# A fixed order for the head of a hybrid encoder layer: one root, rescaling by quarters, idle transposes

## The chip, the cores and the metric

The kernel runs on one core of a Trainium2 chip. The metric is device time in microseconds: 1707.37 before, the median of 3 runs (1707.24 to 1707.54).

## The reference

One layer of a bidirectional encoder, in float32, for one sequence of 256 tokens of width 2048. Cut to what matters:

```python
h = concatenate([meta, x])                  # 16 meta tokens ahead of 256 tokens
n = rms_norm(h, norm_mix)                   # n = h * rsqrt(mean(h*h) + eps) * gain
p = n @ w_in                                # 2048 x 15360: inputs of four mixers, and 4 x 2048 gates
z = [rglru(p_a), hyena(p_b), retention(p_c), hgrn2(p_d)]      # 512 wide each
h = h + sum_b(sigmoid(gate_b) * (z_b @ w_branch_out[b])) @ w_out
h = h + (silu(n2 @ w_gate) * (n2 @ w_up)) @ w_down            # n2 = rms_norm(h, norm_ffn)
return rms_norm(h, norm_final)[16:]
```

The change concerns the first `rms_norm` and its transposition, up to the first projections. Each `rms_norm` needs, for each token, the sum of squares over its 2048 columns, a root and a reciprocal before any column can be scaled.

## The kernel before, in words

All matmuls with weights are done in three passes in a reduced float32 format: weight and activation are each split into a rounded part (`hi`, `nh`) and the rest (`lo`, `nl`), and hi x nh, hi x nl and lo x nh are summed. The weights come from memory in pieces of 128 x 1024 (512 KB), four buffers deep, all on SP's DMA queue, in the order in which `piece` (L95) is called. Of each piece ScalarE (ACT) makes `hi` by a copy (L112) and VectorE (DVE) `lo` by a subtraction (L113); for the first two pieces (`NPOOL`) GpSimd (POOL) does both, 1024 columns at once (L110, L113).

The head works like this. `par` holds all small parameters in one tile of 321 columns and is loaded first (L86); then come the meta tokens `xm`, as 128 rows of 256, and x in two row tiles of 128 tokens, each in two halves of 1024 columns (L226, L231). For the meta tile ACT takes the squares (L260), TensorE (PE) sums them over groups of partitions with the matrix `ind` from `par` (L262), `rsqrt` (L159 to L163) makes the factor in three steps on DVE, ACT and DVE, DVE scales `xm` (L266), PE transposes it (L271), and DVE and ACT write it into `nh` and `nl` (L274, L156, L157). For each row tile `squares` takes the four quarters of 512 columns in turn on ACT and DVE, sums them and takes a root for this tile alone; `rescale` multiplies the quarters in place. Then for each of the 16 column blocks k PE transposes the block of both row tiles into one bank of PSUM (L280), ACT writes `nh[k]` with the gain (L281) and DVE `nl[k]` (L282). The first chunk of the projection (`mix_chunk`) takes pieces 0 to 3, with four blocks k each: 6 matmuls for a block, of 272 columns (L312 to L314).

The order on each engine is not the program's. A planner with its own costs places all instructions: at each moment an engine gets the ready instruction that stands first in the program; the pieces from the seventh on are advanced by 250 places. On the chip each engine then works in this order. Explicit edges without a semaphore (`tc.add_manual_dep`, `tc.issue_after`) put one instruction behind another on the same engine. POOL also issues the DMAs of `mlp` (the inputs of the Hyena filter network, read by `sines` within `filters`, L196) and `rope` (read by `rotate` in mixer C, L688).

Of the kernel before, what the change touches and what calls it, by code (L numbers as in the profile page):

```python
# [10 lines left out]
F32 = mybir.dt.float32  # L11
# [6 lines left out]
P = 128  # L18
D = 2048
# [11 lines left out]
GU_HALF = (6, 5)  # L31
NS, NH, NT = 7, 6, 8
NPOOL = 2
WPAD = 64
WAHEAD = 250
MAGIC = 12582912.0
# [20 lines left out]

PCOL = {}
_n = 0
for _name, _w in (("norm_mix", 16), ("norm_ffn", 16), ("lcw", 16), ("lcb", 4), ("lba", 8), ("lbx", 8), ("lam", 8),  # L60
                  ("hcw", 36), ("hcb", 12), ("hbias", 4), ("lb", 4), ("b1", 1), ("b2", 1), ("dec", 8),
                  ("negt", 2), ("nyq", 1), ("ind", P), ("fill", 48)):
    PCOL[_name] = _n
    _n += _w
NPAR = _n
# [2 lines left out]
def body(tc, a, out):  # L68
# [14 lines left out]
        return psp.tile(list(shape), F32, tag="ps", name=name)  # L83

    par = const.tile([P, NPAR], F32, name="par")
    nc.sync.dma_start(par, a["par"])  # L86

    def pc(name, i=0, rows=P):
        return par[:rows, PCOL[name] + i:PCOL[name] + i + 1]

    ident = const.tile([P, P], F32, name="ident")
    make_identity(nc, ident)

    wpos = [0]
    first = []  # L95

    def piece(kt, cols, dst=None, skip=0):

        i = wpos[0]
        wpos[0] += 1  # L100
        with tc.high_priority(offset=WAHEAD if i >= 6 else 0):
            raw = rawp.tile([P, kt, cols], F32, tag="raw", name="raw")
            nc.sync.dma_start(raw, a["w"][i].rearrange("p (k n) -> p k n", k=kt))
            if dst:
                hi, lo = dst
            else:
                hi, lo = [p.tile([P, 1024 + WPAD], F32R, tag=x, name=x)[:, skip:skip + 1024]
                          .rearrange("p (k n) -> p k n", k=kt) for p, x in ((hip, "hi"), (lop, "lo"))]
            if i < NPOOL:
                G.tensor_scalar(hi, raw, 1.0, 0.0, op0=MUL, op1=ADD)  # L110
            else:
                A.copy(hi, raw)  # L112
            ins = (G if i < NPOOL else V).tensor_tensor(lo, raw, hi.bitcast(F32), op=SUB)  # L113
            if i == 1:
                first.append(ins.ins)
        return hi, lo
# [76 lines left out]


    mlp = H("mlp", 128 + T, rows=64)
    G.dma_start(mlp, a["mlp"])  # L196
    f2 = mc.tile([P, T], F32, name="f2")

    def sine(dst, src, bias):
# [8 lines left out]
        A.activation(dst, x, AF.Sin)  # L208

    def sines():  # L210
        p1 = ps("pf1")
        PE.matmul(p1[:64, :T], mlp[:33, 0:64], mlp[:33, 128:], start=True, stop=True)
        f1 = TT("f1", T, rows=64)
        sine(f1, p1[:64, :T], pc("b1", rows=64))
        p2 = ps("pf2")
        PE.matmul(p2[:64, :T], mlp[:, 64:128], f1, start=True, stop=True)
        sine(f2[:64], p2[:64, :T], pc("b2", rows=64))
        G.memset(f2[64:], 0.0)
# [9 lines left out]
    for t in range(2):  # L228
        halves = [zp.tile([P, 1024], F32, tag=f"z{2 * t + i}", name=f"x{t}_{i}") for i in range(2)]
        for i in range(2):  # L230
            nc.sync.dma_start(halves[i], a["x"][t * P:t * P + P, i * 1024:i * 1024 + 1024])  # L231
        xts.append(halves)
    ss = tiny("ss", 3, 4)
    rs = tiny("rs", 3)

    def quarter(g, q):
        return xts[g][q // 2][:, q % 2 * 512:q % 2 * 512 + 512]

    def squares(g, engs):
        for q, e in enumerate(engs):  # L240
            dump = H("dump", 512)
            x, acc = quarter(g, q), ss[:, g, q:q + 1]
            if e == "A":
                A.activation(dump, x, AF.Square, accum_out=acc)
            else:
                V.scalar_tensor_tensor(dump, x, 1.0, x, op0=MUL, op1=MUL, accum_out=acc)
        r = rs[:, g:g + 1]
        V.tensor_reduce(r, ss[:, g], op=ADD, axis=mybir.AxisListType.X)
        rsqrt(r, r, 1.0 / D)

    def rescale(g, engs):
        for q, e in enumerate(engs):
            x, r = quarter(g, q), rs[:, g:g + 1]
            if e == "A":
                A.activation(x, x, AF.Copy, scale=r)
            else:
                V.tensor_scalar(x, x, r, None, op0=MUL)

    dump = H("dump", 256)
    A.activation(dump, xm, AF.Square, accum_out=ss[:, 2, 0:1])  # L260
    pm = ps("pmeta")
    PE.matmul(pm[:, 0:1], par[:, PCOL["ind"]:PCOL["ind"] + P], ss[:, 2, 0:1], start=True, stop=True)  # L262
    rsqrt(rs[:, 2:3], pm[:, 0:1], 1.0 / D)
    squares(0, "AVAV")
    squares(1, "AVAV")
    V.tensor_scalar(xm, xm, rs[:, 2:3], None, op0=MUL)  # L266
    rescale(0, "AVAV")
    rescale(1, "VAVA")
    pm = ps("pmeta")
    for b in range(2):  # L270
        PE.transpose(pm[:, b * P:b * P + P], xm[:, b * P:b * P + P], ident)  # L271
# [1 line left out]
    gain = par[:, PCOL["norm_mix"]:PCOL["norm_mix"] + KT].rearrange("p (k b) -> p k b", b=2)  # L273
    V.tensor_tensor(nm, pm[:, 0:256].rearrange("p (b t k) -> p k b t", b=2, k=8),  # L274
                    gain[:, :, :, None].to_broadcast([P, 8, 2, META]), op=MUL)
    split(nh[:, :, 0:META], nl[:, :, 0:META], nm.rearrange("p k b t -> p (k b) t"))
    for k in range(KT):
        pt = ps("ptn")
        for t in range(2):
            PE.transpose(pt[:, t * P:t * P + P], xts[t][k // 8][:, (k % 8) * P:(k % 8) * P + P], ident)  # L280
        anchor = [A.activation(nh[:, k, META:], pt[:, :SEQ], AF.Copy, scale=pc("norm_mix", k)),  # L281
                  V.scalar_tensor_tensor(nl[:, k, META:], pt[:, :SEQ], pc("norm_mix", k), nh[:, k, META:].bitcast(F32),  # L282
                                         op0=MUL, op1=SUB)]

    def late(eng, ins):
        tc.add_manual_dep(ins.ins, anchor[eng].ins.name, mybir.DependencyInfo(
# [398 lines left out]

    def mixer_c():
        rope = H("rope", 2, T)
        G.dma_start(rope, a["rope"])  # L688
        def rotate(x, n):

            y = S("rot", NW, n)
# [485 lines left out]
```

## Time and profile before

| | |
|---|---|
| time, median of 3 runs | 1707.37 us |
| the profiled execution | 1708.65 us, span 1706.9 us |
| chain that ended last, by engine | PE 93%, DVE 4%, ACT 2%, issue 1% |
| mean length of a row tile's `nh` (L281) and `nl` (L282) in the first 36 us | 0.475 us each |
| mean length of a piece's `hi` on ACT and `lo` on DVE | 1.05 and 1.24 us |
| first use of `mlp` by PE, of `rope` by DVE | 57.0 and 173.1 us |
| `mlp`, `rope`: from issue to landing | 5.6 and 7.7 us |

The span runs from the first to the last instruction of the profiled execution; what its own time has beyond the span lies ahead of and behind it. A matmul on PE is pipelined, so that the length shown for one is longer than its distance to the next; the chain of waits shows the distances. The granted clock of PE is given as a share of 2.4 GHz.

### The profile page before, as it was taken

The numbers are of one execution on the slowest core, as the hardware profiler recorded it, in microseconds if no ns is written. First come the engines' busy times: TensorE is split into PE (matmuls) and PEld (weight loads), VectorE is DVE, ScalarE is ACT, GpSimd is POOL, SyncE is SP. The second block draws the span as 40 slices with busy tenths as digits, with TensorE's granted clock in tenths as the row PEclk, the third lists the DMA queues.
The fourth block names the chain that finished last, engine by engine and source line by source line (L and its number), as shares of the span: only waits on it lengthen the run. The fifth ranks groups of instructions, "written<-read, shape, count | busy, mean of one in ns | idle before, by whom it ended". The sixth has DMA issues, their size and how long they took to land.

```text
span 1706.9 us, 22379 instructions
## 1 busy us (share of the span) xinstructions
PE 1667.4 (98%) x8844; PEld 1437.0 (84%) x8844; DVE 954.6 (56%) x1140; ACT 803.8 (47%) x969; POOL 80.6 (5%) x74
## 2 busy tenths in 40 slices
PE   6999999999999999999999999999999999999997
PEld 5999999989978888888888888888888888888886
DVE  6755895486675445454455545454545444544554
ACT  5544465474574444444445544444444334444443
POOL 2000000001002002010020000000000000000001
PEclk9999999999999999999999999999999999999999
DMA  6546444546356555555666555555555555555554
GB/s 238 184 140 193 144 140 145 181 139 212 111 172 211 188 194 186 196 194 188 197 198 210 197 197 186 192 190 187 191 190 188 194 196 190 194 185 190 193 191 142
DMA packets 87225, 313.81 MB, mean 184 GB/s; under 512 B 9824, under 2 KB 10112, under 8 KB 86992
## 3 DMA queue, kind: packets, MB, share of 16 engines
q1 hardware_dynamic: 84960, 304.42, 54.0%
q0 software_dynamic: 2160, 7.97, 1.5%
q8 instruction: 69, 1.13, 0.3%
q14 instruction: 36, 0.29, 0.1%
HBM read 309.17 MB, written 2.10 MB: 182 GB/s over the span
## 4 chain that ended last, share of the span: by engine, by line
PE 93%; DVE 4%; ACT 2%; issue 1%; DMA 0%; SPq 0%; ACTq 0%
PE acc L135 23%; PE acc L136 23%; PE acc L134 23%; PE mix L312 5%; PE mix L314 5%; PE mix L313 5%; DVE lo L113 1%; PE pth L948 1%; PE last L1006 1%; PE last L1005 1%; PE last L1007 1%; DMA x<-in_x_dram 0%; ACT hi L112 0%; PE pl L635 0%; PE pg L801 0%
## 5 line engine op out<-in xcount | busy, mean ns | idle before, releaser
L113 DVE TENSOR_TENSOR lo<-raw,hi 128x1024 fp32r<-128x1024 f32 x556 | 686.5, 1235 | 668.9 <-ACT hi L112 668.6
L112 ACT CAST hi<-raw 128x1024 fp32r<-128x1024 f32 x556 | 585.0, 1053 | 759.9 <-PE acc L136 620.1
L136 PE MATMUL acc<-hi,n2l 128*128 128x512 f32 x704 | 274.0, 389 | 0.0
L135 PE MATMUL acc<-lo,n2h 128*128 128x512 f32 x704 | 273.9, 389 | 0.0
L312 PE MATMUL mix<-nh,hi 128*128 128x272 f32 (+2 forms) x896 | 255.0, 287 | 3.4 <-DVE cg L521 1.8
L314 PE MATMUL mix<-nh,lo 128*128 128x272 f32 (+2 forms) x896 | 252.8, 287 | 4.3 <-DVE lo L113 4.3
L313 PE MATMUL mix<-nl,hi 128*128 128x272 f32 (+2 forms) x896 | 255.9, 287 | 0.0
L134 PE MATMUL acc<-hi,n2h 128*128 128x512 f32 x704 | 249.4, 390 | 0.0
L135 PE MATMUL acc<-lo,nh 128*128 128x512 f32 x512 | 200.1, 391 | 2.8 <-DVE lo L113 2.8
L136 PE MATMUL acc<-hi,nl 128*128 128x512 f32 x512 | 199.8, 390 | 0.0
L134 PE MATMUL acc<-hi,nh 128*128 128x512 f32 x512 | 181.7, 391 | 0.6 <-ACT hi L112 0.6
L312 PEld LDWEIGHTS mix<-nh,hi 128*128 128x128 f32 x896 | 169.9, 190 | 5.9 <-issue 2.8
L314 PEld LDWEIGHTS mix<-nh,lo 128*128 128x128 f32 x896 | 168.6, 190 | 6.1 <-DVE lo L113 5.2
L313 PEld LDWEIGHTS mix<-nl,hi 128*128 128x128 f32 x896 | 170.2, 190 | 0.7 <-issue 0.2
L136 PEld LDWEIGHTS acc<-hi,n2l 128*128 128x128 f32 x704 | 132.1, 188 | 27.5
L134 PEld LDWEIGHTS acc<-hi,n2h 128*128 128x128 f32 x704 | 132.2, 188 | 27.1
L135 PEld LDWEIGHTS acc<-lo,n2h 128*128 128x128 f32 x704 | 132.2, 188 | 27.1
L136 PE MATMUL acc<-hi,hidl 128*128 128x512 f32 x312 | 121.4, 389 | 0.0
L135 PE MATMUL acc<-lo,hidh 128*128 128x512 f32 x312 | 121.4, 389 | 0.0
L135 PEld LDWEIGHTS acc<-lo,nh 128*128 128x128 f32 x512 | 96.1, 188 | 24.0 <-DVE lo L113 4.5
L134 PEld LDWEIGHTS acc<-hi,nh 128*128 128x128 f32 x512 | 96.0, 188 | 20.9 <-ACT hi L112 1.3
L136 PEld LDWEIGHTS acc<-hi,nl 128*128 128x128 f32 x512 | 96.2, 188 | 19.6
(388 smaller groups left out, 1644.7 us busy)
## 6 DMA issues: line engine op xcount, KB each, us to landing
raw<-in_w_dram SPq DMA_DIRECT2D x568, 512.0 KB, 3.3
x<-in_x_dram SPq DMA_DIRECT2D x4, 512.0 KB, 8.7
h<-in_x_dram SPq DMA_DIRECT2D x8, 256.0 KB, 4.2
out_dram<-h SPq DMA_DIRECT2D x8, 256.0 KB, 3.1
lruw<-in_lruw_dram POOLq DMA_DIRECT2D x2, 512.0 KB, 6.3
dm<-in_decay_dram POOLq DMA_DIRECT2D x4, 256.0 KB, 4.3
nf<-in_norm_final_dram POOLq DMA_DIRECT2D x1, 1024.0 KB, 6.6
rot<-ck POOLq DMA_DIRECT2D x2, 272.0 KB, 6.0
```

The lines of the kernel that those rows point to most:

```text
L112: A.copy(hi, raw)
L113: ins = (G if i < NPOOL else V).tensor_tensor(lo, raw, hi.bitcast(F32), op=SUB)
L134: PE.matmul(acc[t], xh[:, k, s], wh[:, j], start=(i + j == 0), stop=False)
L135: PE.matmul(acc[t], xh[:, k, s], wl[:, j], start=False, stop=False)
L136: PE.matmul(acc[t], xl[:, k, s], wh[:, j], start=False, stop=(i + j == n - 1))
L312: PE.matmul(o, wh[:, j, s], nh[:, k, t0:T], start=(k == 0), stop=False)
L313: PE.matmul(o, wh[:, j, s], nl[:, k, t0:T], start=False, stop=False)
L314: PE.matmul(o, wl[:, j, s], nh[:, k, t0:T], start=False, stop=(k == KT - 1))
L948: PE.transpose(pt[:, j * P:j * P + P], s[:, j * P:j * P + P], ident)
L1005: PE.matmul(acc, xh, wh, start=(k == 0), stop=False)
L1006: PE.matmul(acc, xh, wl, start=False, stop=False)
L1007: PE.matmul(acc, xl, wh, start=False, stop=(k == 2 * n - 1))
```

## The change

- `par` is loaded in two parts: `norm_mix`, `ind` first (144 columns), the other 177 columns behind x.
- The squares of both row tiles stand ahead of the sum; one reduction and one `rsqrt` serve both. Edges put these steps, on ACT and on DVE, behind the meta tile's split and in program order.
- Row tile 0 is rescaled on ACT, row tile 1 on DVE, by quarters: quarter 0 ahead of the transposes, quarters 1, 2, 3 behind the blocks k = 1, 5, 9. The `nh` and `nl` of all k are held in order with them.
- 40 transposes of the identity into a bank of PSUM that nobody reads stand behind the meta tile's split in the program.
- POOL converts pieces 0 and 1 in four slices of 256 columns each, `hi` and `lo` in turn.
- The conversions of pieces 2, 3, 4 on ACT and DVE are put behind `nh` and `nl` of k = 5, 9, 13.
- The DMA of `mlp` is issued within `filters`, and that of `rope` too behind POOL's last step of piece 1.

```diff
--- before.py
+++ after.py
@@ -31,6 +31,7 @@
 GU_HALF = (6, 5)
 NS, NH, NT = 7, 6, 8
 NPOOL = 2
+NWARM = 40
 WPAD = 64
 WAHEAD = 250
 MAGIC = 12582912.0
@@ -57,9 +58,9 @@
 
 PCOL = {}
 _n = 0
-for _name, _w in (("norm_mix", 16), ("norm_ffn", 16), ("lcw", 16), ("lcb", 4), ("lba", 8), ("lbx", 8), ("lam", 8),
+for _name, _w in (("norm_mix", 16), ("ind", P), ("norm_ffn", 16), ("lcw", 16), ("lcb", 4), ("lba", 8), ("lbx", 8), ("lam", 8),
                   ("hcw", 36), ("hcb", 12), ("hbias", 4), ("lb", 4), ("b1", 1), ("b2", 1), ("dec", 8),
-                  ("negt", 2), ("nyq", 1), ("ind", P), ("fill", 48)):
+                  ("negt", 2), ("nyq", 1), ("fill", 48)):
     PCOL[_name] = _n
     _n += _w
 NPAR = _n
@@ -83,13 +84,21 @@
         return psp.tile(list(shape), F32, tag="ps", name=name)
 
     par = const.tile([P, NPAR], F32, name="par")
-    nc.sync.dma_start(par, a["par"])
+    nc.sync.dma_start(par[:, :PCOL["norm_ffn"]], a["par"][:, :PCOL["norm_ffn"]])
 
     def pc(name, i=0, rows=P):
         return par[:rows, PCOL[name] + i:PCOL[name] + i + 1]
 
     ident = const.tile([P, P], F32, name="ident")
     make_identity(nc, ident)
+
+    last = {}
+    behind = {}
+
+    def after(ins, prev):
+
+        tc.add_manual_dep(ins.ins, prev.ins.name, mybir.DependencyInfo(
+            mybir.DependencyClass.NoSync, mybir.DependencyReason.DATA), reason="order at the head")
 
     wpos = [0]
     first = []
@@ -107,10 +116,19 @@
                 hi, lo = [p.tile([P, 1024 + WPAD], F32R, tag=x, name=x)[:, skip:skip + 1024]
                           .rearrange("p (k n) -> p k n", k=kt) for p, x in ((hip, "hi"), (lop, "lo"))]
             if i < NPOOL:
-                G.tensor_scalar(hi, raw, 1.0, 0.0, op0=MUL, op1=ADD)
+                for j in range(kt):
+                    ins = G.tensor_scalar(hi[:, j], raw[:, j], 1.0, 0.0, op0=MUL, op1=ADD)
+                    if "G" in last:
+                        after(ins, last["G"])
+                    ins = G.tensor_tensor(lo[:, j], raw[:, j], hi[:, j].bitcast(F32), op=SUB)
+                    last["G"] = ins
             else:
-                A.copy(hi, raw)
-            ins = (G if i < NPOOL else V).tensor_tensor(lo, raw, hi.bitcast(F32), op=SUB)
+                ins = A.copy(hi, raw)
+                if i in behind:
+                    after(ins, behind[i][0])
+                ins = V.tensor_tensor(lo, raw, hi.bitcast(F32), op=SUB)
+                if i in behind:
+                    after(ins, behind[i][1])
             if i == 1:
                 first.append(ins.ins)
         return hi, lo
@@ -193,7 +211,6 @@
 
 
     mlp = H("mlp", 128 + T, rows=64)
-    G.dma_start(mlp, a["mlp"])
     f2 = mc.tile([P, T], F32, name="f2")
 
     def sine(dst, src, bias):
@@ -208,6 +225,7 @@
         A.activation(dst, x, AF.Sin)
 
     def sines():
+        G.dma_start(mlp, a["mlp"])
         p1 = ps("pf1")
         PE.matmul(p1[:64, :T], mlp[:33, 0:64], mlp[:33, 128:], start=True, stop=True)
         f1 = TT("f1", T, rows=64)
@@ -230,42 +248,20 @@
         for i in range(2):
             nc.sync.dma_start(halves[i], a["x"][t * P:t * P + P, i * 1024:i * 1024 + 1024])
         xts.append(halves)
+    nc.sync.dma_start(par[:, PCOL["norm_ffn"]:], a["par"][:, PCOL["norm_ffn"]:])
     ss = tiny("ss", 3, 4)
     rs = tiny("rs", 3)
 
     def quarter(g, q):
         return xts[g][q // 2][:, q % 2 * 512:q % 2 * 512 + 512]
 
-    def squares(g, engs):
-        for q, e in enumerate(engs):
-            dump = H("dump", 512)
-            x, acc = quarter(g, q), ss[:, g, q:q + 1]
-            if e == "A":
-                A.activation(dump, x, AF.Square, accum_out=acc)
-            else:
-                V.scalar_tensor_tensor(dump, x, 1.0, x, op0=MUL, op1=MUL, accum_out=acc)
-        r = rs[:, g:g + 1]
-        V.tensor_reduce(r, ss[:, g], op=ADD, axis=mybir.AxisListType.X)
-        rsqrt(r, r, 1.0 / D)
-
-    def rescale(g, engs):
-        for q, e in enumerate(engs):
-            x, r = quarter(g, q), rs[:, g:g + 1]
-            if e == "A":
-                A.activation(x, x, AF.Copy, scale=r)
-            else:
-                V.tensor_scalar(x, x, r, None, op0=MUL)
 
     dump = H("dump", 256)
     A.activation(dump, xm, AF.Square, accum_out=ss[:, 2, 0:1])
     pm = ps("pmeta")
     PE.matmul(pm[:, 0:1], par[:, PCOL["ind"]:PCOL["ind"] + P], ss[:, 2, 0:1], start=True, stop=True)
     rsqrt(rs[:, 2:3], pm[:, 0:1], 1.0 / D)
-    squares(0, "AVAV")
-    squares(1, "AVAV")
     V.tensor_scalar(xm, xm, rs[:, 2:3], None, op0=MUL)
-    rescale(0, "AVAV")
-    rescale(1, "VAVA")
     pm = ps("pmeta")
     for b in range(2):
         PE.transpose(pm[:, b * P:b * P + P], xm[:, b * P:b * P + P], ident)
@@ -273,7 +269,41 @@
     gain = par[:, PCOL["norm_mix"]:PCOL["norm_mix"] + KT].rearrange("p (k b) -> p k b", b=2)
     V.tensor_tensor(nm, pm[:, 0:256].rearrange("p (b t k) -> p k b t", b=2, k=8),
                     gain[:, :, :, None].to_broadcast([P, 8, 2, META]), op=MUL)
-    split(nh[:, :, 0:META], nl[:, :, 0:META], nm.rearrange("p k b t -> p (k b) t"))
+    nm = nm.rearrange("p k b t -> p (k b) t")
+    last["A"] = A.copy(nh[:, :, 0:META], nm)
+    last["V"] = V.tensor_sub(nl[:, :, 0:META], nm, nh[:, :, 0:META].bitcast(F32))
+
+
+    pw_ = ps("pwarm")
+    for i in range(NWARM):
+        PE.transpose(pw_[:, i % 4 * P:i % 4 * P + P], ident, ident)
+
+
+    for t in range(2):
+        for q, e in enumerate("AVAV"):
+            dump = H("dump", 512)
+            x, acc = quarter(t, q), ss[:, t, q:q + 1]
+            if e == "A":
+                ins = A.activation(dump, x, AF.Square, accum_out=acc)
+            else:
+                ins = V.scalar_tensor_tensor(dump, x, 1.0, x, op0=MUL, op1=MUL, accum_out=acc)
+            after(ins, last[e])
+            last[e] = ins
+    V.tensor_reduce(rs[:, 0:2], ss[:, 0:2], op=ADD, axis=mybir.AxisListType.X)
+    rsqrt(rs[:, 0:2], rs[:, 0:2], 1.0 / D)
+
+
+    def rescale(q):
+        for t in range(2):
+            x, r = quarter(t, q), rs[:, t:t + 1]
+            if t == 0:
+                ins = A.activation(x, x, AF.Copy, scale=r)
+            else:
+                ins = V.tensor_scalar(x, x, r, None, op0=MUL)
+            after(ins, last["AV"[t]])
+            last["AV"[t]] = ins
+
+    rescale(0)
     for k in range(KT):
         pt = ps("ptn")
         for t in range(2):
@@ -281,6 +311,13 @@
         anchor = [A.activation(nh[:, k, META:], pt[:, :SEQ], AF.Copy, scale=pc("norm_mix", k)),
                   V.scalar_tensor_tensor(nl[:, k, META:], pt[:, :SEQ], pc("norm_mix", k), nh[:, k, META:].bitcast(F32),
                                          op0=MUL, op1=SUB)]
+        for e, ins in zip("AV", anchor):
+            after(ins, last[e])
+            last[e] = ins
+        if k % 4 == 1:
+            if k < 12:
+                rescale(k // 4 + 1)
+            behind[NPOOL + k // 4 - 1] = anchor
 
     def late(eng, ins):
         tc.add_manual_dep(ins.ins, anchor[eng].ins.name, mybir.DependencyInfo(
@@ -685,7 +722,8 @@
 
     def mixer_c():
         rope = H("rope", 2, T)
-        G.dma_start(rope, a["rope"])
+        with tc.issue_after(first[0]):
+            G.dma_start(rope, a["rope"])
         def rotate(x, n):
 
             y = S("rot", NW, n)
```

## Rows read from the trace of the kernel before

**Rows 1.** The page: busy us (share of the span) and instructions of each engine.
```profile
PE 1667.4 (98%) x8844; PEld 1437.0 (84%) x8844; DVE 954.6 (56%) x1140; ACT 803.8 (47%) x969; POOL 80.6 (5%) x74
```

**Rows 2.** Table of stretches: busy us of each engine, granted clock, DMA share, GB/s.
```profile
18.28:24.10 5.82, 5.80 (x25) 5.43 (x26) 4.87 (x8) 3.24 (x7) 5.68 (x7) 1.00 0.34 93
24.10:204.00 179.90, 179.90 (x1420) 172.90 (x1419) 114.66 (x160) 90.18 (x118) 6.07 (x10) 1.00 0.54 178
204.00:510.00 306.00, 291.40 (x2081) 272.50 (x2080) 217.19 (x382) 182.91 (x258) 8.10 (x16) 0.99 0.47 154
```

**Rows 3.** Chain of waits over the head, in order: start us, us, what.
```profile
13.85 1.24 ACT dump L244 x4
...
15.93 2.31 DVE x L257
...
18.28 1.12 PE ptn L280 x4
...
20.20 0.43 PE ptn L280 x2
...
23.10 0.23 PE mix L314
...
24.18 0.13 PE mix L313
...
24.81 0.22 PE ptn L280 x2
```

**Rows 4.** Timeline of PE around the two rises of its clock.
```profile
22.90 0.43 PE L314 MATMUL mix<-nh,lo 128*128 128x272 f32 x1
...
24.15 0.29 PE L314 MATMUL mix<-nh,lo 128*128 128x272 f32 x1
...
276.14 1.25 PE L512 MATMUL pt<-ident,on 128*128 128x128 f32 x4 [1.85 <-DVE on L509]
278.73 0.59 PE L312 MATMUL mix<-nh,hi 128*128 128x272 f32 x1 [1.34 <-ACT fb L551]
279.12 0.43 PE L313 MATMUL mix<-nl,hi 128*128 128x272 f32 x1
...
283.43 0.30 PE L312 MATMUL mix<-nh,hi 128*128 128x272 f32 x1
```

**Rows 5.** Table of stretches, columns as in rows 2, in the mixers.
```profile
278.00:280.00 2.00, 1.27 (x5) 1.27 (x6) 1.85 (x3) 0.95 (x4) 0.00 (x0) 0.50 0.00 0
```

**Rows 6.** Table of stretches, columns as in rows 2, while x lands.
```profile
2.00:6.00 4.00, 0.58 (x2) 0.50 (x2) 0.32 (x2) 0.93 (x5) 0.82 (x2) 1.00 0.93 212
...
10.00:14.00 4.00, 1.16 (x6) 0.76 (x5) 3.23 (x12) 2.71 (x7) 0.00 (x0) 1.00 1.02 418
```

**Rows 7.** Timeline of the head, all engines: start, us, engine, line, what.
```profile
1.97 0.56 POOL L688 DMA_DIRECT2D rope<-in_rope_dram  x1
...
2.62 0.30 POOL masks.py:199 TENSOR_SCALAR_AFFINE_SELECT ident<-ident 128x128 f32<-128x128 f32 x1
...
5.57 0.17 DVE L163 RECIPROCAL rs<-rs 128x1 f32<-128x1 f32 x1 [0.27 <-ACT rs L162]
...
9.30 0.35 DVE L266 TENSOR_SCALAR xm<-xm,rs 128x256 f32<-128x256 f32 x1
...
9.79 0.66 PE L271 MATMUL pmeta<-ident,xm 128*128 128x128 f32 x2 [4.68 <-DVE xm L266]
...
12.52 1.33 ACT L255 ACTIVATE x<-x,rs 128x512 f32<-128x512 f32 x2 [0.46 <-DVE rs L163]
12.52 0.88 DVE L257 TENSOR_SCALAR x<-x,rs 128x512 f32<-128x512 f32 x2
...
14.23 1.29 POOL L110 TENSOR_SCALAR hi<-raw 128x1024 fp32r<-128x1024 f32 x1 [11.31 <-DMA raw<-in_w_dram]
```

**Rows 8.** Groups of POOL by line: count, busy us, mean ns, idle before.
```profile
L962 POOL TENSOR_TENSOR h<-h,nf 128x512 f32<-128x512 f32 x8 | 12.4, 1566 | 806.1 <-ACT dump L904 806.1
L113 POOL TENSOR_TENSOR lo<-raw,hi 128x1024 fp32r<-128x1024 f32 x2 | 4.8, 2382 | 0.2
```

## The prediction

> **What bounds the kernel now.** I read the page first: TensorE (PE) is busy 98% of the span [rows 1]. Then the table by stretches. From 24.10 to 204 us PE has no idle time at all; from 204 to 510 it is idle 306.0 - 291.4 = 14.6 us, in waits for the token mixers, and nothing the diff edits runs there [rows 2]. So the change can act in one place, the head. What it moves forward there, PE hands on one for one, for there is no idle time behind it to swallow a gain.
>
> Third, the chain of waits over the head [rows 3]. The reader is to see a row of small steps on ACT and DVE that ends in one DVE rescale of 2.31 us at 15.93; PE waits for that and starts its real work, transposes of the row tiles, at 18.28. From there it never pauses.
>
> Fourth, the pitch of the matmuls. In the chain two transposes take 0.43 us at 20.20 and a 128x272 matmul 0.23 at 23.10; from 24.18 on the matmul takes 0.13 and two transposes 0.22 [rows 3]. One matmul by itself lasts 0.43 us at 22.90 and 0.29 at 24.15 [rows 4]. The column of the granted clock reads 1.00 for 18.28 to 24.10 [rows 2], which these lengths contradict: at 278 to 280 us, where it reads 0.50, that is 1.2 of 2.4 GHz, the same matmul again lasts 0.43 [rows 4, 5]. I take 18.28 to 24.1 as PE at the lower level: 5.8 us of work at half speed, 2.9 us lost.
>
> **The change, part by part.**
>
> *DMA ahead of x.* 177 of the 321 columns of par (88 KB of 160.5) go behind x, mlp (100 KB) and rope (272 KB) go behind the second weight piece: 460 KB or 0.47 MB less ahead of x (by the shapes of the tiles). At the 212 GB/s of 2 to 6 us this is 2.2 us, at the 418 GB/s of 10 to 14 us 1.1 us [rows 6]; the DMA engines are busy 0.93 of the one stretch and all of the other, so I take 1.2, near the full one. The first weight piece has landed at 14.23 [rows 7]; 0.524 MB at 418 GB/s before that, at 12.98, the last half of x is there. After: 11.8 (10.8 to 11.9). What is moved comes due late: mlp is first read at 57 us and rope at 173; issued near 22 us, behind POOL's two pieces and among its other loads, they have 30 us and more, where before they took 5.6 and 7.7 from issue to landing. Cost 0; without that time PE would wait about as long as such a load takes.
>
> *One root in place of two, squares first.* Two squares on ACT take 1.24 us, 0.62 each with their read; from the last square's end (15.09) to the rescale's start (15.93) there are 0.84 us: reduce, scale, root, reciprocal [rows 3]. After: 11.8 + 0.75 + 0.84 = 13.4. Tile 0 loses its early start (it was rescaled at 12.52 [rows 7]), but this start was worth only four transposes, since PE then waited for tile 1.
>
> *Rescale by quarters.* Only the first quarter of each tile stands ahead of the first transposes: ACT 0.67 to 0.71 us [rows 7]. DVE's was 2.31 us at 15.93, exactly while GpSimd (POOL) was inside its 2.3 us subtraction; at 12.52, with POOL idle, two took 0.88 [rows 3, 7]. After, POOL's conversion is cut in slices of 256 columns, the first from about 13.2 on and some 0.4 us long, so that DVE ends near 14.05 even if it has to wait for one. First transposes at 13.4 + 0.7 = 14.1, which is 18.28 - 14.1 = 4.2 us sooner. The other three quarters (3 x 0.71 on ACT, 3 x 0.44 to 0.9 on DVE) lie beside PE's work on k = 0 to 3, 24 matmuls of 0.23 us.
>
> *Before had four transposes behind it at 18.28*, done while it waited: at full level 4 x 0.11 = 0.44 us that come back onto the path.
>
> *The early weight pieces behind row tiles.* Pieces 2, 3, 4 are converted on ACT after k = 5, 9, 13. PE reaches them at k = 8, 12 and the next chunk; with 1.05 us of ACT and 1.24 of DVE each (the page) they are ready four row tiles ahead. ACT's supply per k (0.47 us for the row tile, with a share of rescales and pieces (2.8 + 3.2) / 16, some 0.85) stays under PE's demand (6 x 0.1225 + 2 x 0.11 = 0.95). Gain 0, cost 0.
>
> *POOL's slices.* 16 instructions where there were 4. The subtraction took 2.38 us for 1024 columns and 1.57 for 512 [rows 8]: for 256 that is 0.60 in proportion and 1.16 on the line through both. With 0.32 (a quarter of its 1.29) to 0.5 for the copy, a row tile costs POOL 0.92 to 1.66 us, and k = 7 is ready at 20.6 to 26.5. PE gets there at about 24.4 (2.6 row tiles until the clock rises near 20.2, then 0.95 each). I take 1.3 per tile, 23.6: cost 0, at the far end 2.1 us.
>
> *40 idle transposes.* At 0.215 each 8.6 us of PE. They need only the identity, ready at 2.92, or near 1.3 once the two DMA issues ahead of its last step on POOL are gone [rows 7]. The planner fills an idle engine with whatever is ready: rope, which is needed at 173 us, was issued at 1.97. So they run from 1.3 to 3 us on and end near 11, about 3 us before the row tiles. Do they warm? Both rises of the clock came 4.7 us after the first matmul of mix (19.41 to 24.15 and 278.73 to 283.43), while the first transpose lay 5.9 and 7.3 us back [rows 3, 4]; the common delay counts from the matmuls. And a clock once up was down by 278, when PE had done nothing but four transposes in some 4 us [rows 4, 5]. So I take no gain: bounds 0 and 2.9 us; below nothing this can't be but by the order on PE, which is a rival below. The Trainium skill ("TensorE: Matmul & The Clock Gate", "Part 4: PE-mode transpose") says that transposes don't count as PE being busy in the way matmuls do; by it the forecast stands as it is, by the opposite it would be 1700.7, and the trace leans its way without deciding it.
>
> **Sum.** The profiled execution took 1708.65 us (span 1706.9). 4.2 - 0.44 = 3.75 us less: 1704.9. That execution lies 1.28 above the median of the three runs, 1707.37; in the runs' terms 1703.6. Its own range is 1702.6 to 1705.2 (landing 10.8 to 11.9, a rescale blocked by POOL).
>
> **The rivals.**
>
> *The warming works*: the clock is up at 14.1 or soon after. Then up to 2.9 us more, 1700.7. For it: PE is busy for long ahead. Against: the two rises above, and 3 idle us before the first row tile.
>
> *The meta norm stuck behind the idle transposes.* Every square now comes after the meta tile's split on its engine, and that needs PE twice (L262, L271). Before, the reciprocal was there at 5.74, and L271 only came at 9.79 because DVE took a square ahead of the meta scale at 9.30 [rows 7]. Freed: scale 0.35, L271 at 6.1, then 0.66 and three steps on 256 columns of some 0.45 (0.475 for a row tile's, in the table), done at 8.1; four squares of 0.62 must begin by 10.05, so 2.0 us are in hand. But PE works in order. If all 40 stand ahead of L271, it starts at 10.5 to 12.1 (identity, 8.6, and some 0.6 for L262, as for the pair at L271), the squares end at 15.0 to 16.6, the first transposes come at 16.5 to 18.1: a gain of 1.3 to a loss of 0.3, 1706.1 to 1707.7. It decides once more than 21 to 29 of the 40 are planned ahead of L271. The trace can't show how many; it shows that nothing but a ready higher-ranked step stops them.
>
> *POOL as the bound of the first eight row tiles*: the far end above, 1705.7.
>
> *Slower: a second fall of the clock in the mixers.* The order of the whole program is planned anew. At 274.3 PE paused 1.85 and 1.34 us around four transposes, the clock fell and it ran at the lower level to 283.43, some 6.7 us [rows 4, 5]: 3.2 + 3.35 = 6.6 us. One more such place in 204 to 510 gives 1703.6 + 6.6 = 1710.2. It turns the result once new pauses exceed 3.75 us. Against: behind the head only two small DMAs and three conversions change places. The same lot can also take that fall away: 1697.
>
> **How the numbers follow.** Forecast 0.47, warming 0.12, meta behind the transposes 0.20, POOL 0.08, a second fall 0.09, the fall gone 0.04. A measurement tells 0.2%, 3.4 us, from no change; the border is 1703.96, hard by my forecast. Faster: 0.7 of the forecast's 0.47, with the 0.12 and the 0.04, is 0.49. Slower: most of the second fall's upper half, with some allowance, 0.07. Same: 0.44. The range 1700.0 to 1709.0 leaves out the fall gone, the best of the warming and the worst of a second fall, about 0.15.
>
> **What would show it.** Right: first row-tile transpose near 14.1; pitch 0.23 until about 5.8 us after that; no PE pause before 200 us; DVE's first-quarter rescale under 1 us. Wrong: L271 after 8.1 us (the meta rival, and the gain shrinks by what it is late beyond that); a pitch of 0.12 at the first mix (warming); PE waiting for POOL's lo at k = 4 to 7; PE idle between 204 and 510 us more than 1 us off 14.6, or the clock's lower level somewhere else there.

## The result, and the profile after

| | before | after |
|---|---|---|
| median (range), us | 1707.3 (1706.66 to 1707.54), 4 runs | 1697.66 (1697.24 to 1697.99), 4 runs |
| ratio | | 0.9944, 95% interval 0.9927 to 0.9961 |
| profiled execution; its span | 1708.65; 1706.9 | 1697.88; 1696.1 |
| mean granted clock | 0.996 | 0.999 |

The change takes off 9.6 us from median to median and 10.8 from profile to profile; 1703.6 was forecast, with a range that ended at 1700.0. The page of the changed kernel, to hold against [rows 1], shows the 40 idle transposes in PE's count (8884 for 8844) and nothing of where the time went:

```profile
PE 1669.8 (98%) x8884; PEld 1440.3 (85%) x8884; DVE 953.2 (56%) x1137; ACT 802.3 (47%) x968; POOL 82.0 (5%) x86
```

The table of stretches does (busy us of PE, PEld, DVE, ACT, POOL, then granted clock, DMA share, GB/s), to hold against [rows 2]:

```profile
14.50:20.00 5.50, 5.46 (x42) 5.08 (x42) 4.28 (x9) 4.50 (x10) 5.17 (x10) 1.00 0.34 117
20.00:40.00 20.00, 19.51 (x150) 18.35 (x151) 15.70 (x30) 12.17 (x21) 6.87 (x11) 1.00 0.79 269
40.00:204.00 164.00, 163.90 (x1295) 157.26 (x1294) 104.51 (x141) 80.02 (x103) 5.00 (x9) 1.00 0.51 167
204.00:510.00 306.00, 294.40 (x2083) 274.37 (x2082) 217.96 (x379) 183.52 (x256) 8.19 (x16) 1.00 0.49 163
...
274.00:290.00 16.00, 16.00 (x132) 16.00 (x132) 6.97 (x6) 6.32 (x8) 0.00 (x0) 1.00 0.59 195
```

From 204 to 510 us PE is idle for 11.6 us where it was 14.6. The last row is the place of [rows 5]; the same stretch of the kernel before reads:

```profile
274.00:290.00 16.00, 12.81 (x81) 12.00 (x80) 7.77 (x16) 9.14 (x14) 0.00 (x0) 0.79 0.31 97
```

Both kernels run the same 896 matmuls of nh by hi in the mixers' projection (L312, now L349). How much earlier the j-th of them starts than in the kernel before is the **shift**; it tells where time is won along the kernel, and the rest of the text goes by it.

| matmul j | its start before, us | shift, us |
|---|---|---|
| 0 | 19.41 | 5.07 |
| 8 | 25.49 | 7.00 |
| 16 | 29.38 | 5.46 |
| 128 | 73.36 | 5.44 |
| 416 | 196.74 | 5.08 |
| 560 | 265.80 | 2.00 |
| 592 | 286.90 | 10.74 |
| 880 | 499.78 | 10.70 |

So there are two gains: 5.44 us in the head and 5.3 us more between 265 and 287 us. (The dip to 2.00 is other PE work now done ahead of these matmuls, not time lost.)

**The head.** Its timeline after (start, us, engine, line, what; in brackets the idle time before it), to hold against [rows 7]:

```profile
5.81 0.66 PE L267 MATMUL pmeta<-ident,xm 128*128 128x128 f32 x2 [1.17 <-DVE xm L264]
...
6.26 7.21 PE L279 MATMUL pwarm<-ident 128*128 128x128 f32 x40
...
10.53 0.63 ACT L287 ACTIVATE dump<-x 128x512 f32<-128x512 f32 x1 [0.51 <-DMA x<-in_x_dram]
...
12.17 0.64 DVE L302 TENSOR_SCALAR x<-x,rs 128x512 f32<-128x512 f32 x1
...
13.31 1.04 PE L310 MATMUL ptn<-ident,x 128*128 128x128 f32 x8
...
19.32 1.52 DVE L129 TENSOR_TENSOR lo<-raw,hi 128x1024 fp32r<-128x1024 f32 x1 [0.64 <-ACT hi L126]
...
19.73 1.38 POOL L120 TENSOR_SCALAR hi<-raw 128x256 fp32r<-128x256 f32 x1
...
21.16 0.52 PE L349 MATMUL mix<-nh,hi 128*128 128x272 f32 x2 [0.26 <-POOL hi L120]
```

The meta tile's second product (L267) comes at 5.81, ahead of the idle transposes, not behind them. The last quarters of x land at 10.53, the root is done at 12.14, DVE's rescale takes 0.64 us instead of 2.31, and the row tiles start at 13.31: 4.97 us sooner than 18.28. Eight of their transposes take 1.04 us, 0.13 each, so the clock is already up. The chain of waits over the head (start, us, what), to hold against [rows 3], no longer goes over ACT and DVE but over POOL's slices:

```profile
4.26 7.79 DMA raw<-in_w_dram
...
12.13 0.41 POOL hi L120
...
12.61 0.78 POOL lo L123
...
19.76 1.35 POOL hi L120
...
22.38 1.03 POOL lo L123
...
23.45 0.39 PE mix L351
```

PE is held by them at k = 4 to 7: the shift falls from 7.0 at the eighth matmul to 5.46 at the sixteenth. As a sum: 4.97 for the start, 2.9 for the cold stretch that is gone, less 0.44 for the four transposes, less 1.55 for these waits is 5.9, and 5.44 was measured; the remaining 0.4 goes in small gaps before the eighth matmul.

**The mixers.** Before, PE paused 1.85 and 1.34 us there, and the clock was at the lower level from 276.6 to 283.4 [rows 4, 5]. After, one pause of 0.18 is left and the clock stays up. That is 3.0 us of pauses and half of the 5.5 us (6.8 less the 1.34 of idle time in them) that PE worked at the lower level, 2.7. Less the 0.35 that the shift shows as lost near 180 us it makes 5.4, against 5.3 measured.

The cause is the order that the planner made. It has placed the last products of the first pair of HGRN2 heads (po, L716 to L718, L679 to L681 before) 31 to 35 mix matmuls earlier, and the four transposes behind their norm (pt) 20 to 25 earlier, so that 40 mix matmuls instead of 34 lie between and the norm is nearly done when pt comes up. PE's timeline after:

```profile
261.56 0.39 PE L718 MATMUL po<-vtm,sm 128*128 128x128 f32 x2
...
266.84 0.33 PE L549 MATMUL pt<-ident,on 128*128 128x128 f32 x1 [0.18 <-DVE on L546]
```

Before, the last of these products stood at 269.90 and pt at 276.14 [rows 4]. No line of the diff touches either. What lies between them, on PE and ACT, before:

```profile
269.90 0.39 PE L681 MATMUL po<-vtm,sm 128*128 128x128 f32 x2
...
271.39 1.05 ACT L112 CAST hi<-raw 128x1024 fp32r<-128x1024 f32 x1
272.45 1.28 ACT L570 ACT_TABLE_LOAD   x1
...
273.99 1.28 ACT L162 ACT_TABLE_LOAD   x1
275.29 0.20 ACT L162 ACTIVATE rsh<-rsh 128x4 f32<-128x4 f32 x1
```

And after:

```profile
263.15 1.28 ACT L607 ACT_TABLE_LOAD   x1
...
264.69 1.28 ACT L180 ACT_TABLE_LOAD   x1
265.98 0.20 ACT L180 ACTIVATE rsh<-rsh 128x4 f32<-128x4 f32 x1
```

The root of the norm (`rsh`) waits on ACT behind two loads of function tables, 1.28 us each, and before the change behind a weight piece of 1.05 us as well, which the new order puts behind the root. From po to pt 6.2 us pass before (269.90 to 276.14) and 5.3 after (261.56 to 266.84). So the order works from both sides: less between the two on ACT, more work for PE meanwhile. No run parts the two.

### The profile page after: what moved, and what is told of

Read it like the earlier page. It is cut to its first block, busy times and chain, and to the rows that moved or that the text cites. A ratio compares the mean times of both kernels' runs of the same rounds, so it can differ in the third digit from the quotient of the medians.

```text
span 1696.1 us, 22476 instructions
## 1 busy us (share of the span) xinstructions
PE 1669.8 (98%) x8884; PEld 1440.3 (85%) x8884; DVE 953.2 (56%) x1137; ACT 802.3 (47%) x968; POOL 82.0 (5%) x86
## 4 chain that ended last, share of the span: by engine, by line
PE 92%; DVE 4%; ACT 2%; DMA 1%; issue 1%; POOL 1%; SPq 0%; ACTq 0%; DVEq 0%
PE acc L154 24%; PE acc L153 24%; PE acc L152 24%; PE mix L351 5%; PE mix L349 5%; PE mix L350 5%; DVE lo L129 1%; PE pth L986 1%; PE last L1045 1%; PE last L1043 1%; PE last L1044 1%; DMA raw<-in_w_dram 0%; DMA rot<-cq 0%; ACT hi L126 0%; PE pl L672 0%
## 5 line engine op out<-in xcount | busy, mean ns | idle before, releaser
L349 PE MATMUL mix<-nh,hi 128*128 128x272 f32 (+2 forms) x896 | 252.2, 285 | 2.3 <-DVE cg L558 1.8
L349 PEld LDWEIGHTS mix<-nh,hi 128*128 128x128 f32 x896 | 167.8, 188 | 3.8 <-issue 2.1
```

What stands on the lines that cost most here:

```text
L349: PE.matmul(o, wh[:, j, s], nh[:, k, t0:T], start=(k == 0), stop=False)
```

## The experiments

Each was compared with the kernel before on the same chip. "Head" is the shift at j = 127, "mixers" what it gains from there to j = 607, each from one profile of the run against the one profile of before. E5 is the changed kernel once more (1698.1, ratio 0.9945, head 5.47, mixers 5.3), and E9 and E14 are one kernel, so the shifts of a changed kernel repeat to 0.1 us in these two pairs. Medians of one kernel move by up to 0.5, single executions by up to 4 (E2).

The head of the kernel before repeats less well. In E3 every engine has the same order there as before, and yet the first mix matmul comes 0.81 us sooner and the clock rises at 21.64 instead of 24.02: its head is 1.53 us ahead. So how much a head gains over the kernel before is known to some 1.5 us only, while the versions of the changed head can be told apart more finely.

Near 474 us some profiles show a fall of the clock for 3.4 us that costs 0.7 to 0.9 us. It seems to come and go from execution to execution: those of E5 took 1697.8 and 1697.9 at a mean granted clock of 0.999 and 1698.3 twice at 0.997. "Mixers" ends ahead of it.

| run | median, us (n) | ratio, 95% interval | head | mixers |
|---|---|---|---|---|
| after | 1697.66 (4) | 0.9944 [0.9927, 0.9961] | 5.44 | 5.30 |
| E1 no idle transposes | 1698.72 (4) | 0.9947 [0.9932, 0.9962] | 5.73 | 5.13 |
| E2 30 of them | 1705.09 (10) | 0.9983 [0.9973, 0.9993] | 4.34 | -0.26 |
| E3 before, po earlier | 1705.72 (10) | 0.9988 [0.9978, 0.9997] | 1.53 | 1.55 |
| E4 before, with 40 | 1702.57 (6) | 0.9970 [0.9959, 0.9982] | -0.20 | 5.25 |
| E6 half slices | 1697.82 (4) | 0.9943 [0.9928, 0.9958] | 5.48 | 5.67 |
| E7 E6 without the 40 | 1697.99 (4) | 0.9946 [0.9931, 0.9961] | 4.90 | 5.44 |
| E8 no edge to row tiles | 1698.64 (4) | 0.9948 [0.9933, 0.9963] | 4.87 | 5.15 |
| E9, E14 one piece on POOL | 1697.13, 1697.17 (4, 4) | 0.9937 [0.9921, 0.9954], 0.9938 [0.9924, 0.9953] | 6.91, 7.00 | 5.25, 5.26 |
| E10 loads early | 1700.6 (4) | 0.9956 [0.9941, 0.9970] | 3.78 | 5.55 |
| E11 whole pieces on POOL | 1698.89 (4) | 0.9946 [0.9931, 0.9961] | 5.61 | 5.34 |
| E12 two roots | 1697.96 (4) | 0.9942 [0.9927, 0.9957] | 5.42 | 5.43 |
| E13 E9 without the 40 | 1698.56 (4) | 0.9947 [0.9930, 0.9963] | 5.14 | 5.11 |

### Is the second gain the order, or the warming?

**E1**, no idle transposes.
```diff
-NWARM = 40
+NWARM = 0
```


> The changed kernel without the 40 idle transposes; all else as changed, and in the order planned for PE the output products of the first HGRN2 pair still stand early (from mix matmul 1659 on). Theory W (the transposes raise the clock): the rise moves from 11.7 us to some 5.7 us after the first row-tile transpose at 13.3, near 19.0; the first mix matmuls lie 0.23 us apart; 2.9 us are lost, less what PE then no longer waits for POOL (up to 1.75): 1698.8 to 1700.6. Rival (transposes do not count for the clock, something else raised it early): the rise stays near 11.7 and the time at 1697.7.

The gain in the mixers stays, and by the shift the head loses nothing, where a loss of 1.1 to 2.9 us was expected: the order theory holds so far, and the 40 transposes are worth nothing in this head. (The median is 0.6 to 1.1 us above E5 and the changed kernel; the profile has the fall near 474 us.) They do warm, though. PE's timeline of E1, where the rise comes 3.9 us after the first row tile:

```profile
12.93 1.97 PE L310 MATMUL ptn<-ident,x 128*128 128x128 f32 x8 [6.63 <-ACT x L300]
...
16.50 0.43 PE L350 MATMUL mix<-nl,hi 128*128 128x272 f32 x1
16.73 0.35 PE L351 MATMUL mix<-nh,lo 128*128 128x272 f32 x1
16.92 0.29 PE L350 MATMUL mix<-nl,hi 128*128 128x272 f32 x1
```

The eight transposes take 1.97 us instead of 1.04, but they start 0.38 us sooner, because the 40 still occupy PE until 13.31 in the changed kernel; and what PE does faster when warm it waits for at POOL's slices later.

**E2**, the count alone changed: a planner's order that is late again would bring the pauses back.
```diff
-NWARM = 40
+NWARM = 30
```


> The changed kernel with 30 idle transposes in place of 40. The planner then puts the output products of the first HGRN2 pair behind mix matmul 1694, as in the kernel before, and not at 1659. Theory O (that order makes the pause of PE and the fall of the clock near 276 us): the head keeps its 5.4 us, the pause and the fall are back and cost 5.3: 1703.0 (1702.3 to 1703.6). Rival (the pause went because data land earlier or the clock is up from the start, whatever the order): 1697.7, no pause over 1 us between 255 and 285.

The late order came (products 31 to 35 mix matmuls later), and with it all of the loss. PE's waits from 250 to 295 us (total, times, longest) in the changed kernel:

```profile
PE pt L549 <- DVE on L546: 0.2, 1, 0.2
```

The same waits in E2:

```profile
PE pt L549 <- DVE on L546: 1.9, 1, 1.9
PE mix L349 <- ACT fb L588: 1.5, 1, 1.5
```

And E2's table of stretches, with the clock going down:

```profile
270.00:272.00 2.00, 0.21 (x1) 0.14 (x1) 0.80 (x4) 1.97 (x3) 0.00 (x0) 1.00 0.81 258
272.00:274.00 2.00, 0.89 (x4) 0.41 (x3) 0.71 (x3) 1.99 (x5) 0.00 (x0) 0.72 0.01 4
274.00:276.00 2.00, 1.62 (x7) 1.62 (x8) 2.00 (x4) 0.94 (x4) 0.00 (x0) 0.50 0.00 0
```

This is [rows 4, 5] over again, 7.4 us for ten instructions fewer: by the shift 1.1 in the head, 5.6 in this place, and 0.7 at a fall near 481 us. It is 2 us more than expected, since the head lost too, all of it between the eighth and the sixteenth matmul, where POOL's slices end at 24.62 instead of 23.41. The ten times lie between 1702.6 and 1706.6.

**E3**, the kernel before with one edge: the 1635th mix matmul waits for the last of the products, so that they are early.
```diff
+                    if nmix[0] == 1635:
+                        tc.add_manual_dep(ins.ins, pins["po"].name, mybir.DependencyInfo(
+                            mybir.DependencyClass.NoSync, mybir.DependencyReason.DATA), reason="po first")
```


> The kernel before with one edge more: a mix matmul waits in PE's order for the last output product of the first HGRN2 pair, so that these products stand at mix matmul 1668 instead of 1694; the head is untouched. Theory O: the pause of 1.85 us at 276 and the fall of the clock go: 5 to 6.6 us less, 1700.7 to 1702.3. Rival (the order is not the cause): the wait only changes its place, 1706 to 1708.

A miss: the mixers gain 1.55 us of the 5.3, and the head's 1.53 is no work of the edit (above). The pause at pt went (0.18 us), but a wait of 1.73 us for DVE's q came behind it, and the clock fell for 3.4 us. PE's waits in E3 over the same stretch:

```profile
PE mix L315 <- DVE q L528: 1.7, 1, 1.7
PE mix L321 <- DVE lo L113: 0.3, 1, 0.3
PE pt L519 <- DVE on L516: 0.2, 1, 0.2
```

Only the products were moved; in the changed kernel pt too stands some 20 mix matmuls earlier. Moving one step by hand does not give the planner's order.

**E4**, the kernel before with the 40 idle transposes, which changes the plan and leaves the head's work as it was.
```diff
+    pw_ = ps("pwarm")
+    for i in range(40):
+        PE.transpose(pw_[:, i % 4 * P:i % 4 * P + P], ident, ident)
```


> The kernel before with the 40 idle transposes behind the meta tile's split and nothing else. The plan has the early order in the first HGRN2 pair (1659). Theories W and O together: the transposes run from 10.5 to about 18, the clock is up by 18.3 (2.9 us) and the pause is gone (5.3): 1699.1 (1698.3 to 1700.5). O without W: 1702.0. W without O: 1704.4. Neither: 1707.3.

The order is the early one, both pauses and the fall are gone, and the mixers gain 5.25 with a head that gains nothing. That settles the second gain: it needs no faster head, only the other plan. In medians it is 4.75 us, with an interval of 3.1 to 7.0, and the time is near that of "O without W". In the head the transposes raised the clock at 13.6, but PE then waited 1.78 us for DVE's rescale of x and the level fell at 20.4, when the row tiles had hardly used it (table of stretches of E4):

```profile
16.00:18.00 2.00, 1.18 (x11) 0.94 (x9) 1.94 (x2) 1.33 (x2) 1.92 (x2) 1.00 0.18 74
18.00:20.00 2.00, 0.82 (x6) 0.62 (x6) 2.00 (x2) 0.68 (x2) 1.92 (x3) 1.00 0.20 47
20.00:22.00 2.00, 1.91 (x9) 1.68 (x10) 1.79 (x6) 2.00 (x5) 2.00 (x1) 0.61 0.57 221
22.00:24.00 2.00, 2.00 (x11) 2.00 (x11) 2.00 (x3) 0.68 (x2) 1.94 (x5) 0.54 0.05 1
```

Which plan one gets follows no size: with 0 to 20 and 36 to 44 idle transposes the changed kernel's program has the early order, with 24, 30, 48 and 52 the late one (read from the programs; only 0, 30 and 40 were run).

### What holds PE in the head?

**E6 and E7**, the second piece in slices of 512 columns; E7 also without the 40.
```diff
-                for j in range(kt):
-                    ins = G.tensor_scalar(hi[:, j], raw[:, j], 1.0, 0.0, op0=MUL, op1=ADD)
+                n = 1 if i == 0 else 2
+                for j in range(0, kt, n):
+                    ins = G.tensor_scalar(hi[:, j:j + n], raw[:, j:j + n], 1.0, 0.0, op0=MUL, op1=ADD)
...
+                    ins = G.tensor_tensor(lo[:, j:j + n], raw[:, j:j + n], hi[:, j:j + n].bitcast(F32), op=SUB)
```


> The changed kernel with piece 0 on POOL in four slices as changed, but piece 1 in two slices of 512 columns. Theory P (with the clock up, PE waits for POOL's slices of piece 1 at k = 4 to 7, some 1.75 us in all): the waits shrink to under 0.5 us, 1.2 to 1.7 us less than the changed kernel: 1696.0 to 1696.6. Rival (PE is held by ACT and DVE there, not by POOL): the same time as the changed kernel, within 0.4.

> As e6_half, and without the idle transposes. Theory P and W: now that POOL does not hold PE, a late rise of the clock costs its half: the cold stretch from 13 us to 17 or 19 makes 1.8 to 2.9 us, 1698.0 to 1699.5. Rival (the warming is worth nothing here in any case): as e6_half, within 0.5.

No gain in E6, against the forecast: fewer instructions for POOL, but the last subtraction took 2.12 us beside one of DVE's, 1.29 for the one before it. The timeline of POOL in E6:

```profile
18.13 1.29 POOL L124 TENSOR_TENSOR lo<-raw,hi 128x512 fp32r<-128x512 f32 x1
19.39 0.80 POOL L121 TENSOR_SCALAR hi<-raw 128x512 fp32r<-128x512 f32 x1
20.27 2.12 POOL L124 TENSOR_TENSOR lo<-raw,hi 128x512 fp32r<-128x512 f32 x1
```

Here warming is worth 0.6 us in the head (5.48 against 4.90), less than the 1.8 to 2.9 of the forecast; the medians differ by 0.2.

**E8**, no edge from the early pieces to row tiles.
```diff
-            behind[NPOOL + k // 4 - 1] = anchor
```


> The changed kernel without the edges that put the conversions of pieces 2, 3, 4 behind the row tiles k = 5, 9, 13; ACT and DVE take them where the planner puts them. By my prediction (PE is the bound there, the edges are worth nothing): the same as the changed kernel, within 0.5. Rival (a conversion ahead of a row tile holds PE, as at 20 us in the kernel before): PE waits for nh or nl once or twice, 1 to 2 us more.

The edges are worth 0.6 us, between the two forecasts. Without them ACT and DVE convert piece 2 2.6 us sooner (15.67 for 18.24), in the middle of POOL's slices, and PE's longest wait for POOL's hi, at 22.15, is 0.70 us.

**E9 and E14**, one piece on POOL instead of two, the other four on ACT and DVE behind row tiles.
```diff
-NPOOL = 2
+NPOOL = 1
...
-            if i == 1:
+            if i == 0:
                 first.append(ins.ins)
...
+        if k in {3: 1, 6: 2, 10: 3, 13: 4}:
+            behind[{3: 1, 6: 2, 10: 3, 13: 4}[k]] = anchor
```


> The changed kernel with only piece 0 on POOL, in slices; piece 1 goes to ACT and DVE behind k = 3, pieces 2, 3, 4 behind k = 6, 10, 13. The order in the first HGRN2 pair stays early (1659). Theory Q (the head is held at k = 4 to 8 by POOL and DVE taking turns at their common memory port; without POOL's second piece both are free): PE's waits between 14.5 and 25 us fall from some 1.7 to under 0.7: 1696.3 to 1697.2. Rival (DVE is the bound and gets 1.2 us more to do): 1698.0 to 1699.5.

> e9_pool_one once more, beside e13. Head gain 6.9 us and 12.2 behind the first HGRN2 pair; 1696.3 to 1697.5, the higher end where the clock falls near 475 us as in the profile of e9.

The second part of the edit puts rope's DMA behind POOL's last step of piece 0. POOL was what held PE: with half its work gone the eighth matmul's shift of 7.2 is still 7.0 at the sixteenth, and the head gives 6.9 to 7.0 us. This is the fastest version run, in both runs 0.5 us under the changed kernel's median and 0.9 to 1.0 under E5's, with intervals of the ratio that overlap; its profiles have the fall near 474 us that the changed kernel's lack, so less than the 1.5 us of the head arrives. Its table of stretches (E14), PE without a gap:

```profile
14.50:20.00 5.50, 5.50 (x45) 5.21 (x44) 5.04 (x11) 5.30 (x10) 5.29 (x11) 1.00 0.41 140
20.00:40.00 20.00, 20.00 (x161) 19.44 (x160) 15.53 (x29) 13.15 (x21) 0.83 (x2) 1.00 0.86 283
```

**E13**, E9 without the 40.
```diff
-NWARM = 40
+NWARM = 0
```


> As e9_pool_one, without the idle transposes; early order in the first HGRN2 pair. Theory H (the warming is worth its half of the cold stretch, but only where nothing else holds PE): the head's gain falls from 6.9 to 5.0 to 5.7 us, the time is 1.2 to 1.9 us above e9_pool_one. Rival (the warming is worth nothing at all, the matmuls of the head are not what bounds it): within 0.4 of e9_pool_one at the fourth chunk.

Now that POOL no longer holds PE, warming is worth 7.00 - 5.14 = 1.9 us of the head, and 1698.56 against 1697.17 in the times of the same chip, as theory H has it. Not all of the distance to E7's 0.6 has to come from POOL: the clock rose 5.5 us after the first row tile here (18.54 less 13.01), 4.0 in E7, and half of this difference is 0.8 us.

**E10**, mlp and rope issued at the start, as before the change.
```diff
+    G.dma_start(mlp, a["mlp"])
...
-        with tc.issue_after(first[0]):
-            G.dma_start(rope, a["rope"])
+        G.dma_start(rope, a["rope"])
```


> The changed kernel with the DMAs of mlp and rope issued at the start, as before; par stays in two parts. Theory D (what lands ahead of x sets the start): x lands 0.9 to 1.2 us later, the first row-tile transpose comes near 14.3 instead of 13.2 and the head's gain falls by as much: 1698.5 to 1699.3. Rival (the start is set by the chain of squares and root, or PE waits for POOL anyway): 1697.7 to 1698.1.

The last quarters of x land at 11.35 instead of 10.53 and the first row tile comes at 13.76, only 0.45 later, since the 40 transposes hid the rest; but the first weight piece is late by the same 0.8 us and POOL starts its slices at 12.96, so the head loses 1.7, of which 1.1 by PE's waits for POOL. It is the largest loss of the parts taken out of the changed kernel one by one. The median lies 1.3 us above the forecast: the profiled execution (1699.27) bears out the shift, the other three took 1700.6 to 1700.9, and no trace shows why.

**E11**, whole pieces on POOL.
```diff
-                for j in range(kt):
-                    ins = G.tensor_scalar(hi[:, j], raw[:, j], 1.0, 0.0, op0=MUL, op1=ADD)
...
+                G.tensor_scalar(hi, raw, 1.0, 0.0, op0=MUL, op1=ADD)
+                ins = G.tensor_tensor(lo, raw, hi.bitcast(F32), op=SUB)
```


> The changed kernel with POOL's two pieces whole again: a copy and a subtraction of 1024 columns each. By the slices' purpose: DVE's first rescale waits for a copy of 1.3 us, first transposes near 14.0, the first lo is ready only at 15.9 and PE waits 1 us for it, but POOL ends piece 1 about 2 us sooner and PE's later waits go: 1697.3 to 1698.8. Rival (slices only cost POOL time): 1696.5.

The slices are worth nothing: 5.61 whole, 5.44 sliced (the time has the fall near 475 us in it). Whole, PE waits early, for the first piece's lo at 15.91; sliced, it waits late, because a piece costs POOL 4.75 us (four times 1.19) instead of 3.6, before any wait for DVE. The timeline of E11:

```profile
13.44 2.42 POOL L120 TENSOR_TENSOR lo<-raw,hi 128x1024 fp32r<-128x1024 f32 x1
...
15.91 0.39 PE L347 MATMUL mix<-nh,lo 128*128 128x272 f32 x1 [0.42 <-POOL lo L120]
```

**E12**, a root for each row tile.
```diff
-    V.tensor_reduce(rs[:, 0:2], ss[:, 0:2], op=ADD, axis=mybir.AxisListType.X)
+    for t in range(2):
+        V.tensor_reduce(rs[:, t:t + 1], ss[:, t], op=ADD, axis=mybir.AxisListType.X)
```


> The changed kernel with a sum and a root for each row tile again, both behind all squares; the rest as changed. The second root's steps (about 0.2 us each on DVE, ACT, DVE, and the sum) come behind the first's: row tile 1 is rescaled 0.4 to 0.8 us later, and so is the first pair of transposes: 1698.1 to 1698.6. Rival (hidden behind PE's waits at k = 4 to 7): 1697.7 to 1698.0.

The first transposes come not later but 0.67 us sooner (12.64; 0.47 sooner than in E5), since row tile 0 no longer waits for the sum over both (ACT's first rescale stands at 11.88 for 12.17), and the head ends where it was (5.42): one root in place of two is worth nothing that can be measured, since POOL decides here too.

## Why the prediction was wrong

**The step that failed** is "nothing the diff edits runs there" of 204 to 510 us, with "behind the head only two small DMAs and three conversions change places". True of the source, false of the program: the planner orders all of it anew, and the new order took the two pauses and the fall of the clock away, 5.3 us. E2 shows it from the other side: with 30 transposes and the late order the changed kernel takes 1705.09, inside the range. The prediction had this as the lower half of a rival, at 0.04, and its size (6.6) counted the pause inside the fall twice; E4 gives 5.25 for it alone. That its 1697 lies so near the 1697.66 measured is luck: 1.3 too much for the fall, 1.7 too little for the head (5.44 for 3.75). The rows to see it by were there: a pause of 1.85 us in a plan written for one set of lengths is an accident that any new plan can undo or make.

**Term by term:**
- *Start.* 4.2 forecast, 4.97 measured. x landed at 10.53, below the lower end of 10.8; from there squares, root and rescale took what was worked out (12.89 without a wait, 14.1 less the 1.3). 0.4 us of it went to the idle transposes, still on PE until 13.31. Why x landed so early is not fully shown: E10 puts 0.8 us to mlp and rope. And against the head of E3, which starts 0.81 us sooner, the 4.97 would be 4.2.
- *Idle transposes.* "They run from 1.3 to 3 us on and end near 11": they ran from 6.26, behind L267, which also took the rival "meta norm stuck" away. "I take no gain": the clock was up at the first row tile, which is 2.9 us. That the rise counts from the mix matmuls, read from two rises, was wrong: it came at 11.74, ahead of the first of them at 14.34. Yet the net worth in this kernel is nothing (E1), 0.6 in E7 and 1.9 in E13, because the time went to the next wait. So "no gain" was right by luck, and "the warming works" right as a mechanism and wrong as a time.
- *POOL's slices.* 0 forecast, 1.55 measured by the shift. POOL had k = 7 ready at 23.41, near the forecast (23.6), in part by luck: it began 1.1 us sooner (12.13 for 13.2), and its tiles took 1.41 in the mean for 1.3, 1.19 where DVE did not hold them. But PE was not at 24.4: with the clock up and the earlier start it got there first. The cover was PE's slowness, and other terms of the same sum took it.
- *Edges behind row tiles.* 0 forecast, 0.6 measured (E8).
- *mlp and rope moved.* 1.2 for all the DMA moved, par's columns among it; 1.7 for these two alone, two thirds of it over POOL's later start. That they cost nothing where they now stand was right: PE is idle for 0.1 us from 40 to 204.
- *Rescale by quarters* was right: 0.64 on DVE for 2.31.

## What to carry to other kernels

Where a planner orders the whole program, a change at the head is a new draw for every near miss behind it: look in the profile before for the pauses that the order alone decides, price them both ways (here 5.3 us, about as much as the whole head), and give them a real chance. Terms of a sum that each make one engine sooner share the next wait: after adding them up, walk that engine forward and ask what it now reaches too early, as here POOL's slices. Warming an engine pays only as far as nothing else holds it in the time that is won (0, 0.6 and 1.9 us in three versions of the same head, one profile each without the warming). And before a gain is read from one profile of the old kernel, look how far two executions of the same order lie apart: here 1.53 us in the head.

## What the runs showed of the hardware

**Transposes raise the clock.** Idle transposes per 2 us in the changed kernel, when PE did nothing else (table of stretches, that line alone: PE busy, granted clock, DMA share, GB/s):

```profile
7.00:9.00 2.00, 2.00 (x11) 1.00 1.01 393
9.00:11.00 2.00, 2.00 (x12) 1.00 1.05 417
11.00:13.00 2.00, 2.00 (x17) 1.00 1.02 418
```

The pitch goes from 0.22 to 0.11 us (the rise is at 11.74 here, 8.81 in E5), while the column reads 1.00 throughout: ahead of the first change on record it is no measure. The Trainium skill ("TensorE: Matmul & The Clock Gate", "Part 4: PE-mode transpose") says that a transpose doesn't count as PE being busy the way a matmul does; this trace, with transposes in float32, does not agree.

**DVE and POOL block each other.** Alone, POOL's copy of 256 columns takes 0.40 us and DVE's subtraction of 1024 takes 1.24; at 19.3 to 21.1 us of the changed kernel, side by side, they took 1.38 and 1.52, and before the change DVE's rescale, 0.44 with POOL idle, took 2.31 beside POOL's subtraction [rows 3, 7]. The Trainium skill ("SBUF — State Buffer", "SBUF: two separate sides") describes a pair of ports that one of the two engines holds for a whole instruction while the other waits; the trace agrees as far as the waiting goes, since the copy, begun beside the subtraction, ended only 0.27 us behind it (21.11 and 20.84). The ports themselves no trace shows.
